# Attention of the first group: scores eight steps ahead of their unit's transposes instead of six

## The chip, the cores and the metric

The kernel runs on one core of a Trainium2 chip. The metric is the device time of one execution in microseconds (us); the median of three runs before the change is 1029.18 us (1029.17 to 1029.4).

## The reference

One layer of a transformer over 1024 tokens of width 1024, all in float32. Two groups of heads share one input projection. Group A is windowed attention with grouped keys and a sink per head, group B is neighbourhood attention on a 16 x 64 grid. After them come an output projection and a gated MLP with a depthwise convolution of width 3.

```python
hn = rmsnorm(h, norm_mix[l])
proj = jnp.einsum('bsd,de->bse', hn, w_in[l])
qa, ka, va, qb, kb, vb = jnp.split(proj, splits, axis=-1)
...
# group A, per block of 128 queries: keys of the blocks before, at and after it
s = jnp.einsum('bqgrd,bkgd->bgrqk', q_i, k_i).astype(jnp.float32) * scale
s = jnp.where(valid[None, None, None], s, -1e30)
m = jnp.maximum(jnp.max(s, axis=-1), sink_gr)
p = jnp.exp(s - m[..., None])
denom = jnp.sum(p, axis=-1) + jnp.exp(sink_gr - m)
o = jnp.einsum('bgrqk,bkgd->bgrqd', p.astype(v_i.dtype), v_i)
...
mix = jnp.concatenate([rmsnorm(o_a, norm_a[l]), rmsnorm(o_b, norm_b[l])], axis=-1)
h = h + jnp.einsum('bse,ed->bsd', mix, w_out[l])
hn = rmsnorm(h, norm_ffn[l])
h = h + conv_gated_mlp(hn, w_gate[l], w_up[l], conv_w[l], conv_b[l], w_down[l])
```

Group A has 8 query heads and 2 heads of keys and values, 64 wide, so four query heads share a key head.

## The kernel before

Activations lie with features on the partitions and tokens along the free axis. Every large product is done as three matmuls on operands split into a high and a low part in a rounded format (`x` is high plus low): high by high, high by low and low by high. These three are one **block** (`block`, L177 to L179, into `pj`); a projection job has 16 blocks, eight for each half of the tokens. TensorE's instructions run in the order in which the program writes them (`manual_schedule`); those of the other engines are put in order by a planner, by priorities and its own model of time, and each engine then runs its queue in that order.

**Filling.** The generator `rest` yields one block at a time of the input projections 3 to 17 and then of the output projection; `fill(n)` writes n blocks. While attention runs, such blocks are written between its steps, so that TensorE has work while VectorE, ScalarE and GpSimd do the softmax. `RATES` says how many blocks go to each stretch of eight units of group A, or of four units of group B.

**Units of group A.** A unit (`unit_window`) is one of two key heads by one of eight blocks of 128 tokens: 16 units. It has four score steps (`q_step`, one for each query head) and two or three transposing steps (`t_step`, one for each block of keys, two for the blocks at the ends). In what follows units are counted from one: the first, the second, and so on.

- A score step writes two matmuls into one of two PSUM banks with tag `s` (L389). VectorE reads the bank, adds the mask and takes the extreme (L412, with `nm` as the result); ScalarE takes the exponential and its sum (L416). Two scores make a pair in one tile `p`. After the second one VectorE takes the reciprocals (L418) and GpSimd scales both halves (L420). GpSimd has before that copied the sinks into two columns of the tile (L411).
- A transposing step takes one block of keys out of all four scores of the unit: four transposes (L452) into a bank with tag `pt`. ScalarE writes its high part `ph` (L426) and VectorE the rest `pl` (L427). The product with the values (L457 with `ph`, L458 with `pl`, into `o`) is written one transposing step later.

Pairs lie in seven tiles in turn: five of tag `p` in the attention pool, and, for the pairs numbered 3 and 6 of each seven (`SPARE`), two of tag `mix` (`pair_tile`).

**The order around the change.** `q_until(u, limit)` hands out the next score steps in order, up to unit u and at most `limit` of them. `FILL0` = 22 blocks are written before any score. Then a first part writes `4 + AHEAD` scores (the first unit's four and `AHEAD` of the second unit's), each followed by one or two blocks in turn, and then a tail of blocks. With six scores this is 9 blocks among them and `FILL1 - 9` = 5 behind them, 14 in all. Then the units take turns. In a unit's turn its transposing steps and products alternate, and four further score steps are put in at the places `EVA` = (1, 3, 5, 8), with blocks after each event. Each such turn of units 1 to 14 takes four scores, so the scores stay the same number ahead of the transposes; from the 15th unit on, all scores up to two units ahead are taken, whatever their number. `run_q` writes blocks beyond the rate if a unit's projections have not been finished when its score is due.

Of the kernel before, what the change touches and what calls it, by code (L numbers as in the profile page):

```python
# [32 lines left out]
FILL0, FILL1 = 22, 14  # L33
RATES = [41, 50, 21, 21, 21, 21, 13, 19, 20, 17]
SPARE = (3, 6)
AHEAD = 2
EVA = (1, 3, 5, 8)
WARM = 8

# [17 lines left out]
def hybrid_layer(tc, xT, w_first, w_in, w_out, w_gate, w_up, w_down, small, sink, rpb, consts, rope, out):  # L57
    nc = tc.nc
    with ExitStack() as ctx:
# [765 lines left out]
        def fill(n):  # L825
            while n > 0 and next(filler, False):
                n -= 1
# [27 lines left out]
        def q_until(u, limit):  # L855
            nonlocal qpos
            res = []
            while qpos < len(queue_q) and queue_q[qpos][0] <= u and len(res) < limit:
                res.append(queue_q[qpos])
                qpos += 1  # L860
            return res

        def run_q(items):
            for u, s in items:
                while any(m not in done for m in flat[u][2]):
                    assert next(filler)
                s()
# [14 lines left out]
        pend = None  # L882
        for i, item in enumerate(q_until(1, 4 + AHEAD)):
            run_q([item])
            fill(i % 2 + 1)
        fill(FILL1 - 9)
        for u in range(len(flat)):
            q, t, need, kind = flat[u]
            if kind == 0 and u < 14:
# [719 lines left out]
```

## Time and profile before

| What | us |
|---|---|
| median of three runs | 1029.18 |
| profiled execution, its own time | 1030.14 |
| its span, from the first to the last instruction | 1028.4 |
| TensorE (PE) busy in the span | 1011.9 |
| VectorE (DVE) busy | 836.6 |
| ScalarE (ACT) busy | 560.6 |
| GpSimd (POOL) busy | 107.7 |

The first scores of group A start at 54 us, its last transposes at 182 us; group B's attention follows up to about 354 us, then the output projection and the MLP. In rows of the profile an instruction is given by its start in us, its length in us, engine, line of the program, operation, output and inputs with their shapes, and `x` with the number of instructions joined in the row. Brackets at the end hold the idle time of the engine before the row, and what released it. A row of a window gives its busy time for PE, PEld (loading of weights), DVE, ACT and POOL, each with a count, then the granted clock of TensorE, the share of DMA and GB/s. SyncE (SP) here only issues DMA. In the table of waits a row says who waited for whom, the total in us, how often, and the longest.

### The profile page before, as it was taken

To read this page: it belongs to the slowest core of one execution; us is meant where nothing else is said; L and a number is where in the kernel's file an instruction comes from. 1 tells how busy PE (TensorE), PEld (TensorE's weight loads), DVE (VectorE), ACT (ScalarE), POOL (GpSimd) and SP (SyncE) were. 2 spreads that over 40 slices of the span, in tenths; PEclk is the share of its full clock that TensorE was granted. 3 is DMA by queue.
4 is the path that set the end of the run, shared out by engine and by line. 5 is a ranking of instruction groups with operands and counts; after the bars stand their busy time and mean duration, and the time that the engine had idled before them with its cause. 6 is when DMAs were issued, how large, how long until landed. Compare 5 with 4: busy or idle time off the path is not lost.

```text
span 1028.4 us, 14846 instructions
## 1 busy us (share of the span) xinstructions
PE 1011.9 (98%) x5094; PEld 889.3 (86%) x5094; DVE 836.6 (81%) x1566; ACT 560.6 (55%) x1077; POOL 107.7 (10%) x188
## 2 busy tenths in 40 slices
PE   9999999999999999999999999999999999999996
PEld 8888888888888888888888888888888888888886
DVE  7889888768888799999987777786787767896765
ACT  8467776657676545565545444443544644554451
POOL 0233332232242100000000000000000000000002
PEclk9999999999999999999999999999999999999998
DMA  7223122333325247313443332233322889866644
GB/s 291 77 77 78 47 72 62 84 81 82 83 61 176 76 164 261 102 50 114 154 185 103 124 121 95 102 113 113 102 111 95 285 281 305 299 237 236 225 149 164
DMA packets 68220, 144.94 MB, mean 141 GB/s; under 512 B 8240, under 2 KB 18736, under 8 KB 68144
## 3 DMA queue, kind: packets, MB, share of 16 engines
q1 hardware_dynamic: 58064, 118.82, 36.0%
q10 hardware_dynamic: 10080, 25.17, 6.3%
q8 instruction: 40, 0.66, 0.3%
q14 instruction: 36, 0.29, 0.1%
HBM read 103.58 MB, written 28.57 MB: 129 GB/s over the span
## 4 chain that ended last, share of the span: by engine, by line
PE 77%; DVE 13%; ACT 4%; DMA 3%; issue 2%; SPq 0%; POOL 0%; DVEq 0%; ACTq 0%; POOLq 0%
PE dn L994 6%; PE dn L992 6%; PE dn L993 6%; PE x L992 6%; PE x L993 6%; PE x L994 6%; PE pj L177 5%; PE pj L178 5%; PE pj L179 5%; PE y L992 3%; PE y L993 3%; PE y L994 3%; PE s L389 3%; PE z L993 2%; PE z L992 2%
## 5 line engine op out<-in xcount | busy, mean ns | idle before, releaser
L992 PE MATMUL x<-hg,whi 128*128 128x512 f32 x352 | 133.7, 380 | 1.2 <-ACT gs L1034 1.2
L993 PE MATMUL x<-hg,whi 128*128 128x512 f32 x352 | 133.4, 379 | 0.0
L994 PE MATMUL x<-hg,wlo 128*128 128x512 f32 x352 | 133.4, 379 | 0.0
L992 PE MATMUL dn<-xd,whi 128*128 128x512 f32 (+1 forms) x330 | 120.8, 366 | 0.0
L993 PE MATMUL dn<-xd,whi 128*128 128x512 f32 (+1 forms) x330 | 120.5, 365 | 0.0
L994 PE MATMUL dn<-xd,wlo 128*128 128x512 f32 (+1 forms) x330 | 120.5, 365 | 0.0
L416 ACT ACTIVATE p<-p,nm 128x385 f32<-128x385 f32 (+3 forms) x128 | 74.9, 586 | 53.8 <-DVE nm L412 50.3
L177 PE MATMUL pj<-xgh,whi 128*128 128x512 f32 x245 | 99.9, 408 | 0.7 <-ACT xgh L637 0.4
L966 ACT ACTIVATE whi<-ws 128x512 fp32r<-128x512 f32 (+1 forms) x100 | 60.7, 621 | 71.9 <-DVE ws L1106 16.5
L420 POOL TENSOR_SCALAR p<-p,sm 128x384 f32<-128x384 f32 (+1 forms) x128 | 78.7, 628 | 198.9 <-DVE sm L418 159.4
L178 PE MATMUL pj<-xgl,whi 128*128 128x512 f32 x245 | 93.0, 379 | 0.3 <-DVE xgl L638 0.3
L179 PE MATMUL pj<-xgh,wlo 128*128 128x512 f32 x245 | 92.9, 379 | 0.0
L966 ACT ACTIVATE whi<-raw 128x512 fp32r<-128x512 f32 (+1 forms) x102 | 60.9, 611 | 44.1 <-PE x L993 20.0
L967 DVE TENSOR_TENSOR wlo<-ws,whi 128x512 fp32r<-128x512 f32 (+1 forms) x100 | 66.6, 679 | 20.1 <-ACT whi L966 19.9
L427 DVE TENSOR_TENSOR pl<-pt,ph 128x384 fp32r<-128x384 f32 (+2 forms) x108 | 63.3, 589 | 20.5 <-ACT ph L426 18.3
L1314 ACT ACTIVATE xd<-xd 128x512 fp32r<-128x512 f32 x77 | 47.5, 626 | 54.5 <-DMA xd<-x 54.0
L992 PEld LDWEIGHTS x<-hg,whi 128*128 128x128 f32 x352 | 66.5, 189 | 11.4 <-ACT gs L1034 2.0
L1315 DVE TENSOR_TENSOR xd<-xd 128x512 fp32r<-128x512 f32 x77 | 52.2, 686 | 29.6 <-ACT xd L1314 29.3
L1429 POOL TENSOR_TENSOR h<-h,wide 128x256 f32<-128x256 f32 (+1 forms) x6 | 5.4, 915 | 672.0 <-ACT wide L1425 672.0
L994 PEld LDWEIGHTS x<-hg,wlo 128*128 128x128 f32 x352 | 66.5, 189 | 9.4
L993 PEld LDWEIGHTS x<-hg,whi 128*128 128x128 f32 x352 | 66.5, 189 | 9.4
L992 PEld LDWEIGHTS dn<-xd,whi 128*128 128x128 f32 x330 | 62.5, 189 | 7.7
(267 smaller groups left out, 2531.7 us busy)
## 6 DMA issues: line engine op xcount, KB each, us to landing
xd<-x SPq DMA_DIRECT2D x77, 256.0 KB, 5.3
raw<-in_w_down_dram SPq DMA_DIRECT2D x72, 256.0 KB, 4.1
raw<-in_w_gate_dram SPq DMA_DIRECT2D x22, 512.0 KB, 3.5
raw<-in_w_up_dram SPq DMA_DIRECT2D x22, 512.0 KB, 3.5
x<-c ACTq DMA_DIRECT2D x22, 512.0 KB, 2.6
raw<-in_w_in_dram SPq DMA_DIRECT2D x30, 256.0 KB, 2.8
raw<-in_w_down_dram SPq DMA_DIRECT2D x36, 192.0 KB, 4.4
x<-t ACTq DMA_DIRECT2D x11, 512.0 KB, 2.6
```

The costliest lines, as they stand in the source:

```text
L177: nc.tensor.matmul(ps, w[0], mv(x[0][:, tsl(h)]), start=first, stop=False)
L178: nc.tensor.matmul(ps, w[0], mv(x[1][:, tsl(h)]), start=False, stop=False)
L179: nc.tensor.matmul(ps, w[1], mv(x[0][:, tsl(h)]), start=False, stop=last)
L416: nc.scalar.activation(p[:, j, 0:e], p[:, j, 0:e], AF.Exp, bias=nm, scale=-1.0, accum_out=sm[:, j:j + 1])
L420: nc.gpsimd.tensor_scalar(p[:, i, 0:m], p[:, i, 0:m], sm[:, i:i + 1], 1.0, op0=ALU.mult, op1=ALU.mult)
L427: mark["rest"] = nc.vector.tensor_tensor(pl[:, 0:n], ps[:, 0:n], f32(ph[:, 0:n]), op=ALU.subtract)
L966: nc.scalar.activation(hi, src, AF.Copy)
L967: nc.vector.tensor_tensor(lo, src, f32(hi[:, :, :]), op=ALU.subtract)
L992: nc.tensor.matmul(ps, w[0], x[0], start=first and i == 0, stop=False, skip_group_check=True)
L993: nc.tensor.matmul(ps, w[0], x[1], start=False, stop=False, skip_group_check=True)
L994: nc.tensor.matmul(ps, w[1], x[0], start=False, stop=last and i == len(ws) - 1, skip_group_check=True)
L1315: nc.vector.tensor_tensor(lo, f32(lo), f32(hi), op=ALU.subtract)
```

## The change

`AHEAD` goes from 2 to 4, so the first part writes eight scores, the first and the second unit's, and each unit's turn writes scores that lie eight steps ahead of its own transposes. The first part then has 12 blocks among its scores, and the tail behind it is cut from five blocks to two, so that 14 blocks are written before the first transposes as before. No instruction is added or taken away.

```diff
-AHEAD = 2
+AHEAD = 4
...
         for i, item in enumerate(q_until(1, 4 + AHEAD)):
             run_q([item])
             fill(i % 2 + 1)
-        fill(FILL1 - 9)
+        fill(FILL1 - 12)
         for u in range(len(flat)):
             q, t, need, kind = flat[u]
             if kind == 0 and u < 14:
```

## The prediction

> **What bounds the kernel now.** I read the page first, then the busy time by stages, the waits of TensorE, and last the engines' instructions in order of time around every stop of TensorE in the first group's attention (54 to 182 us).
>
> ```profile
> span 1028.4 us, 14846 instructions
> PE 1011.9 (98%) x5094; PEld 889.3 (86%) x5094; DVE 836.6 (81%) x1566; ACT 560.6 (55%) x1077; POOL 107.7 (10%) x188
> 60.00:70.00 10.00, 10.00 (x58) 8.97 (x57) 7.59 (x20) 5.91 (x14) 4.21 (x7) 1.00 0.35 98
> 100.00:110.00 10.00, 9.08 (x51) 7.53 (x51) 9.60 (x28) 8.06 (x23) 4.12 (x8) 1.00 0.44 106
> 110.00:120.00 10.00, 10.00 (x62) 9.00 (x61) 7.58 (x26) 6.56 (x20) 3.17 (x9) 1.00 0.08 27
> 54.00:182.00 128.00, 126.62 (x716) 112.73 (x716) 110.06 (x321) 90.83 (x233) 44.78 (x91) 1.00 0.25 67
> PE pt L452 <- POOL p L420: 0.8, 2, 0.6
> PE s L389 <- DVE nm L412: 0.5, 1, 0.5
> ```
>
> Rows by window give window, length, then busy us of PE, PEld, DVE, ACT and POOL, the granted clock, and DMA. TensorE's stream is written out by hand and it is busy 98% of the span at a clock of 1.00, so the time can move only by what TensorE now loses by waiting. The change keeps every matmul, so the whole question is the stops. In the first group's 128 us TensorE is idle for only 128.00 - 126.62 = 1.38 us. The waits of 60 to 110 us name two causes: transposes (L452) that wait for GpSimd's scaling of `p` (L420), and one score that waits for VectorE to read its bank.
>
> Idle time understates a stop here, because a matmul's shown end overlaps the next start. So I take stops from the distance between starts:
>
> ```profile
> 98.85 0.60 PE L452 MATMUL pt<-cst,p 128*128 128x128 f32 x4
> 99.21 0.41 PE L389 MATMUL s<-ka,q 128*128 128x384 f32 x1
> ...
> 100.70 0.38 PE L452 MATMUL pt<-cst,p 128*128 128x128 f32 x2
> 101.68 0.33 PE L452 MATMUL pt<-cst,p 128*128 128x128 f32 x1 [0.60 <-POOL p L420]
> 102.24 0.33 PE L452 MATMUL pt<-cst,p 128*128 128x128 f32 x1 [0.23 <-POOL p L420]
> 102.33 0.46 PE L177 MATMUL pj<-xgh,whi 128*128 128x512 f32 x1
> ...
> 108.92 0.91 PE L452 MATMUL pt<-cst,p 128*128 128x128 f32 x4
> 109.58 0.46 PE L177 MATMUL pj<-xgh,whi 128*128 128x512 f32 x1
> 130.49 0.80 PE L452 MATMUL pt<-cst,p 128*128 128x128 f32 x4
> 131.05 0.41 PE L389 MATMUL s<-ka,q 128*128 128x384 f32 x1
> 154.08 0.79 PE L452 MATMUL pt<-cst,p 128*128 128x128 f32 x4
> 154.63 0.46 PE L177 MATMUL pj<-xgh,whi 128*128 128x512 f32 x1
> ```
>
> Four transposes that find their input ready take 99.21 - 98.85 = 0.36 us. The first four of the sixth unit take 102.33 - 100.70 = 1.63, a loss of 1.27. The same sum at 108.92, 130.49 and 154.08 (first transposes of the seventh, tenth and thirteenth unit) gives 0.66, 0.56 and 0.55, losses of 0.30, 0.20 and 0.19. Together 1.96 us: everything that the wait for scaled `p` costs in this group.
>
> The Trainium skill, "Perfetto Trace Analysis", section Tensor Engine Instruction, says the end of a TensorE instruction is computed by the profiler and not observed. The trace agrees: by the idle column the first stop is 0.60 + 0.23 = 0.83 us, by starts 1.27, and the three others do not appear as idle at all; a sum by idle time alone would stop at 0.83.
>
> Why the sixth unit waits is read backwards from 100.70:
>
> ```profile
> 97.28 0.60 DVE L412 CUSTOM_DVE_ANT_0 p<-s,cst,nsink 128x384 f32<-128x384 f32 x1
> 99.73 0.61 ACT L416 ACTIVATE p<-p,nm 128x385 f32<-128x385 f32 x1
> 100.79 0.16 DVE L418 RECIPROCAL sm<-sm 128x2 f32<-128x2 f32 x1
> 95.59 1.15 POOL L420 TENSOR_SCALAR p<-p,sm 128x384 f32<-128x384 f32 x2 [2.99 <-DVE sm L418]
> 101.04 1.15 POOL L420 TENSOR_SCALAR p<-p,sm 128x384 f32<-128x384 f32 x2 [1.45 <-DVE sm L418]
> ```
>
> The reduce of the unit's fourth score starts at 97.28, its exponential at 99.73 (ScalarE did other work first), the reciprocal at 100.79, and the scaling of the pair ends at 101.04 + 1.15 = 102.19, when the transposes have already stood for over a microsecond. The row at 95.59 scales the pair before it.
>
> **The change, part by part.** *Steady part.* Each unit's turn still issues four scores at the same four places of the stream; two complete a pair each, at the same places as before. So each engine has the same work at the same place; only the pair it belongs to is later by one. The last pair of a unit is therefore scaled where its first pair is scaled now: for the sixth unit by 95.59 + 1.15 = 96.74 and not 102.19, 3.96 us ahead of the transposes at 100.70. All four losses go: -1.96 us.
>
> *What is late next.* VectorE is busy 9.60 of 10 us where the first two stops lie and has no room to follow a faster TensorE there:
>
> ```profile
> 101.92 0.69 DVE L427 TENSOR_TENSOR pl<-pt,ph 128x512 fp32r<-128x512 f32 x1
> 103.60 0.38 PE L458 MATMUL o<-pl,v 128*128 128x512 f32 x1
> 109.31 0.68 DVE L427 TENSOR_TENSOR pl<-pt,ph 128x512 fp32r<-128x512 f32 x1
> 110.75 0.38 PE L458 MATMUL o<-pl,v 128*128 128x512 f32 x1
> ```
>
> The product at 103.60 needs the rest `pl` that ends at 101.92 + 0.69 = 102.61, a margin of 0.99. TensorE would arrive 1.27 earlier and wait 0.28; it carries 0.99 on. The stop at 108.92 adds 0.30, so 1.29. The product at 110.75 needs the `pl` that ends at 109.99: margin 0.76, so 0.53 more goes back and 0.76 is left. From 110 to 120 VectorE is busy only 7.58 of 10 us, so nothing more is taken, and 0.20 + 0.19 at the later stops are kept. Net: -1.96 + 0.28 + 0.53 = -1.15 us. Bounds: nothing given back, -1.96; all of the first two stops given back, -0.39. I take the middle value since both margins are read from rows, though VectorE's order may shift by an instruction.
>
> *Prelude.* Two scores (the second unit's last) move ahead of the first transposes, with the three filling blocks that stood in the tail of five. Before the first transposes there are 14 blocks either way: 9 + 5 before, 12 + 2 after. The two scores bring two reduces, two exponentials, a reciprocal and a scaling ahead of the first `ph` and `pl`:
>
> ```profile
> 62.45 0.17 DVE L418 RECIPROCAL sm<-sm 128x2 f32<-128x2 f32 x1 [0.78 <-ACT p L416]
> 66.09 0.29 DVE L265 TENSOR_TENSOR f<-f,turns 128x128 f32<-128x128 f32 x1 [1.43 <-DMA f<-t]
> 66.16 0.60 ACT L426 ACTIVATE ph<-pt 128x512 fp32r<-128x512 f32 x1 [2.56 <-PE pt L452]
> ```
>
> VectorE stands idle for 0.78 and 1.43 us there and ScalarE for 2.56. Two reduces at 0.60 (the row at 97.28) and a reciprocal at 0.16 make 1.36, inside 2.21; two exponentials at 0.61 make 1.22, inside 2.56. TensorE loses nothing in 60 to 70 us (10.00 of 10). So 0. If that cover were gone, 1.36 us of VectorE work would stand before the first `pl`: between 0 and +1.36. I take 0, since the idle stands just where the scores would land.
>
> *The one wait of a score, in the third unit's turn.* Reduces per unit are unchanged, so I keep it. Bounds: -0.46 (its idle) to 0.
>
> ```profile
> 80.98 0.43 PE L389 MATMUL s<-ka,q 128*128 128x384 f32 x1 [0.46 <-DVE nm L412]
> ```
>
> *Buffers and the end of the group.* Pairs live in seven tiles, five of tag `p` and two spare. At most five were in use at once; now six. A pair takes the tile of the pair seven before it, whose last transposes now lie half a unit nearer, but still in the unit before: 0. In the fifteenth unit two scores are left for four, since the second group's first two are issued earlier; the projections that the ninth unit and the second group need are done by block count well before (by block 52 where 66 have run, and by 84 where 114 have), so no block is pulled forward: 0. No score of this group issues a DMA, and no transfer changes its place on SyncE's queue.
>
> *A port rule, weighed.* GpSimd's scaling meets VectorE:
>
> ```profile
> 107.86 1.58 POOL L420 TENSOR_SCALAR p<-p,sm 128x384 f32<-128x384 f32 x2 [3.33 <-PE pt L452]
> 102.52 0.68 DVE L170 TENSOR_TENSOR wlo<-raw,whi 128x512 fp32r<-128x512 f32 x1
> 108.07 0.91 DVE L170 TENSOR_TENSOR wlo<-raw,whi 128x512 fp32r<-128x512 f32 x1
> ```
>
> The scaling of two at 107.86 took 1.58 and not 1.15, and the weight split that began inside it 0.91 and not 0.68. One such meeting more costs VectorE 0.23, which is within the bounds above. The Trainium skill, "SBUF — State Buffer", section Who interferes with whom, says a VectorE instruction with two SBUF inputs and a GpSimd instruction that reads SBUF block one another. It speaks against moving scalings; by it the sum would be at worst -1.15 + 2 x 0.23 = -0.69 if both pairs moved ahead in the prelude met a split there.
>
> **Sum.** The profiled execution took 1030.14 us (a span of 1028.4 and 1.74 around it), 0.96 above the median of the runs, 1029.18. Against its own time: 1030.14 - 1.15 = 1028.99. For the median: 1029.18 - 1.15 = 1028.03, so 1028.0, with -1.96 to -0.39, 1027.2 to 1028.8, as this case's own range.
>
> **Rivals.** *More than the sum:* nothing is given back and the score's wait goes too, since two reduces are done early: -1.96 - 0.46 = -2.42, 1026.8. For it: VectorE's 2.21 us of idle are used before its busy stretch. Against: its work per unit stays, and both margins above are too short.
>
> *The lead is only on paper:* VectorE's lag simply moves to another wait. All of the first two stops comes back (-0.39), and the prelude's cover fails (+1.36): up to +0.97, 1030.2. For it: 9.60 of 10 us busy. Against: 7.58 just after.
>
> *Slower, by GpSimd's queue.* Its queue runs in order and holds the sink copies (L411), which wait for a tile to be freed by transposes:
>
> ```profile
> 68.42 1.27 POOL L411 COPY p<-nsink 128x2 f32<-128x2 f32 x2 [4.57 <-PE pt L452]
> 69.67 1.15 POOL L420 TENSOR_SCALAR p<-p,sm 128x384 f32<-128x384 f32 x2
> 92.29 0.31 POOL L411 COPY p<-nsink 128x2 f32<-128x2 f32 x2
> ```
>
> At 68.42 a copy stood 4.57 us for transposes with a scaling behind it. With six of seven tiles in use, the copy waits for a unit's last transposes; scalings queued behind it start only then. From the fifth unit's last transposes (98.85) to the sixth's first (100.70) lie 1.85 us: room for 0.36 of transposes, 0.31 of copies and one scaling of a pair, 1.15 (1.82). It decides from the second pair behind a copy: 0.36 + 0.31 + 2.30 - 1.85 = 1.12 lost per unit. In six of the twelve units from the third on that is 6.7 - 2.0 = +4.7, 1033.9; from four units (4.5 - 2.0 = +2.5) it is slower by over 0.2%. Against it: a pair has a unit's time before it is needed, and the planner has so far put copies where nothing urgent stands behind.
>
> **How the numbers follow.** 0.2% of 1029.18 is 2.06 us, about what a measurement of this kernel can tell from no change. Forecast (-0.39 to -1.96) 0.47; more than the sum 0.18, faster; only on paper 0.16; slower by GpSimd's queue 0.19. So faster 0.18, within 0.2% 0.63, slower 0.19. The range goes from 1026.7 to 1030.2 (the three first cases, the low end widened by 0.1, since idle understates the score's wait) and leaves out the last.
>
> **What would show it.** Right: the first transposes of the sixth, seventh, tenth and thirteenth unit follow in 0.36 us and the wait of L452 for L420 is gone; a wait of `o` for `pl` (L458 on L427) appears at the sixth or seventh unit; 60 to 70 us stays at 10.00 busy; the wait of L389 at the third unit stays. Wrong: L452 still waiting for GpSimd, with L411 ahead of L420 in its queue; idle before 70 us; or a difference after 190 us, where I expect the same stream shifted by one constant.

## The result and the profile after

The changed kernel took 1027.84 us (median of 22 runs), the kernel before 1029.36 us (median of 22 runs beside them). The ratio is 0.9985, with a 95% interval of 0.9978 to 0.9991: 1.5 us faster (0.9 to 2.3). On another occasion the same kernel gave 0.9981 (0.9972 to 0.9989). The forecast was 1028.0 in 1026.7 to 1030.2, and within 0.2% of the time before.

The profiled execution of the changed kernel took 1027.14 us, 3.0 less than that of before. This pair of profiles overstates the gain: the two differ at the start and in the MLP, which also differ between repeats of one kernel. From the first matmul of L992, in the MLP, to the end the changed kernel took 611.9 us in one profile and 612.8 in another. The attention does not have this scatter, so the experiments below are read there.

The busy time by stages of the changed kernel, and then the waits of TensorE (50 to 110 us; us in total, times, longest):

```profile
60.00:70.00 10.00, 10.00 (x58) 9.05 (x58) 8.41 (x24) 6.83 (x17) 3.69 (x7) 1.00 0.37 103
100.00:110.00 10.00, 9.90 (x59) 8.66 (x58) 9.11 (x31) 8.09 (x22) 4.88 (x10) 1.00 0.30 77
54.00:182.00 128.00, 127.75 (x725) 114.09 (x724) 110.41 (x327) 92.77 (x238) 44.35 (x91) 1.00 0.25 66
```

```profile
PE s L389 <- DVE nm L412: 0.2, 1, 0.2
```

TensorE's idle time from 54 to 182 us fell from 1.38 to 0.25 us. The wait of L452 for GpSimd's L420 is gone from the table. In 60 to 70 us VectorE is busy 8.41 us where it was 7.59: the two scores that moved ahead. TensorE lost nothing there.

The first transposes of the sixth, seventh, tenth and thirteenth unit, and what follows them, in TensorE's instructions in order of time; and GpSimd's scaling of the sixth unit's last pair:

```profile
101.05 0.60 PE L452 MATMUL pt<-cst,p 128*128 128x128 f32 x4
101.41 0.46 PE L177 MATMUL pj<-xgh,whi 128*128 128x512 f32 x1
...
107.79 0.60 PE L452 MATMUL pt<-cst,p 128*128 128x128 f32 x4
108.15 0.46 PE L177 MATMUL pj<-xgh,whi 128*128 128x512 f32 x1
...
129.63 0.60 PE L452 MATMUL pt<-cst,p 128*128 128x128 f32 x4
129.98 0.41 PE L389 MATMUL s<-ka,q 128*128 128x384 f32 x1
...
153.25 0.60 PE L452 MATMUL pt<-cst,p 128*128 128x128 f32 x4
153.61 0.46 PE L177 MATMUL pj<-xgh,whi 128*128 128x512 f32 x1
95.87 1.16 POOL L420 TENSOR_SCALAR p<-p,sm 128x384 f32<-128x384 f32 x2 [2.85 <-DVE sm L418]
```

All four take 0.35 or 0.36 us, where they took 1.63, 0.66, 0.56 and 0.55. The pair that the sixth unit waited for is scaled by 95.87 + 1.16 = 97.03, 4.0 us ahead of its transposes (3.96 were forecast). The whole 1.96 us of this wait went.

What came in its place, again in TensorE's order, with the VectorE instruction behind each:

```profile
80.67 0.38 PE L458 MATMUL o<-pl,v 128*128 128x512 f32 x1
80.92 0.43 PE L389 MATMUL s<-ka,q 128*128 128x384 f32 x1
...
89.15 0.60 PE L452 MATMUL pt<-cst,p 128*128 128x128 f32 x4
89.90 0.43 PE L389 MATMUL s<-ka,q 128*128 128x384 f32 x1 [0.15 <-DVE nm L412]
89.23 0.61 DVE L412 CUSTOM_DVE_ANT_0 p<-s,cst,nsink 128x384 f32<-128x384 f32 x1
...
109.10 0.38 PE L457 MATMUL o<-ph,v 128*128 128x512 f32 x1
109.58 0.48 PE L458 MATMUL o<-pl,v 128*128 128x512 f32 x1
109.90 0.38 PE L177 MATMUL pj<-xgh,whi 128*128 128x512 f32 x1
108.84 0.68 DVE L427 TENSOR_TENSOR pl<-pt,ph 128x512 fp32r<-128x512 f32 x1
...
148.69 0.60 PE L452 MATMUL pt<-cst,p 128*128 128x128 f32 x4
149.25 0.43 PE L389 MATMUL s<-ka,q 128*128 128x384 f32 x1
...
174.97 0.46 PE L457 MATMUL o<-ph,v 128*128 128x512 f32 x1
175.36 0.48 PE L458 MATMUL o<-pl,v 128*128 128x512 f32 x1
175.68 0.38 PE L177 MATMUL pj<-xgh,whi 128*128 128x512 f32 x1
```

The score's wait of the third unit's turn is nearly gone: 80.92 - 80.67 = 0.25 for a step of 0.22. Four new stops stand against it, all for VectorE by what they follow:

- 89.90 - 89.15 = 0.75 less 0.36, so 0.39: a score whose bank is read by the reduce at 89.23.
- 109.58 - 109.10 = 0.48 less 0.22, so 0.26: the product for the `pl` that ends at 109.52. The step behind it is longer too, 109.90 - 109.58 = 0.32 for 0.22, so 0.36 in all.
- 149.25 - 148.69 = 0.56 less 0.36, so 0.20: a score again.
- 175.68 - 174.97 = 0.71 for the two products behind a group of transposes, where the same place takes 0.51 in the kernel with eight steps and no scaling (below), so 0.20. The `pl` of this product ends at 175.30.

Together 1.15 us.

Beyond the first group there is one more difference, at the second transposes of the next values, with the kernel before first and the changed kernel second:

```profile
186.36 0.60 PE L334 MATMUL vt<-cst,t 128*128 128x128 f32 x4
187.30 0.45 PE L177 MATMUL pj<-xgh,whi 128*128 128x512 f32 x1 [0.34 <-DVE v L339]
```

```profile
184.88 0.60 PE L334 MATMUL vt<-cst,t 128*128 128x128 f32 x4
185.32 0.45 PE L177 MATMUL pj<-xgh,whi 128*128 128x512 f32 x1
```

The distance fell from 187.30 - 186.36 = 0.94 to 0.44 us, another 0.50; undisturbed it would be 0.36. After it the two streams run at a constant distance through the rest of attention.

### The profile page after: what moved, and what is told of

It reads as the page before. It is cut to its first block, busy times and chain, and to the rows that moved or that the text cites. A ratio compares the mean times of both kernels' runs of the same rounds, so it can differ in the third digit from the quotient of the medians.

```text
span 1025.3 us, 14859 instructions
## 1 busy us (share of the span) xinstructions
PE 1011.5 (99%) x5094; PEld 890.5 (87%) x5094; DVE 836.6 (82%) x1566; ACT 562.0 (55%) x1077; POOL 108.6 (11%) x188
## 4 chain that ended last, share of the span: by engine, by line
PE 84%; DVE 10%; ACT 4%; issue 2%; DMA 1%; DVEq 0%; POOL 0%; ACTq 0%; POOLq 0%
PE dn L994 7%; PE dn L992 7%; PE dn L993 6%; PE pj L177 6%; PE pj L178 6%; PE pj L179 6%; PE x L992 6%; PE x L993 6%; PE x L994 6%; PE y L994 3%; PE y L993 3%; PE y L992 3%; PE s L389 3%; PE z L994 2%; PE z L992 2%
## 5 line engine op out<-in xcount | busy, mean ns | idle before, releaser
L992 PE MATMUL x<-hg,whi 128*128 128x512 f32 x352 | 133.6, 380 | 0.9 <-ACT gs L1034 0.9
L992 PE MATMUL dn<-xd,whi 128*128 128x512 f32 (+1 forms) x330 | 120.8, 366 | 0.0
L420 POOL TENSOR_SCALAR p<-p,sm 128x384 f32<-128x384 f32 (+1 forms) x128 | 79.7, 635 | 204.6 <-DVE sm L418 177.8
L992 PEld LDWEIGHTS x<-hg,whi 128*128 128x128 f32 x352 | 66.5, 189 | 10.9 <-ACT gs L1034 1.5
L992 PEld LDWEIGHTS dn<-xd,whi 128*128 128x128 f32 x330 | 62.5, 189 | 7.7
```

The costliest lines, as they stand in the source:

```text
L420: nc.gpsimd.tensor_scalar(p[:, i, 0:m], p[:, i, 0:m], sm[:, i:i + 1], 1.0, op0=ALU.mult, op1=ALU.mult)
L992: nc.tensor.matmul(ps, w[0], x[0], start=first and i == 0, stop=False, skip_group_check=True)
```

## The experiments

For a comparison free of the scatter at the start I take the distance between two marks that every kernel has: the first value transposes of all, near 60 us, and those near 222 us. Here they are for the kernel before, then for the changed one:

```profile
60.76 1.04 PE L334 MATMUL vt<-cst,t 128*128 128x128 f32 x8
223.85 0.60 PE L334 MATMUL vt<-cst,t 128*128 128x128 f32 x4
```

```profile
60.63 1.04 PE L334 MATMUL vt<-cst,t 128*128 128x128 f32 x8
221.88 0.60 PE L334 MATMUL vt<-cst,t 128*128 128x128 f32 x4
```

That is 163.09 and 161.25 us. The same difference for each kernel, beside the ratio of its times to the kernel before run beside it:

| kernel | between the marks | against 163.09 | time ratio (95%) |
|---|---|---|---|
| before, again | 163.14 | +0.05 | 1.0000 (0.9991 to 1.0009) |
| changed | 161.25 | -1.84 | 0.9985 (0.9978 to 0.9991) |
| changed, again | 161.17 | -1.92 | 0.9981 (0.9972 to 0.9989) |
| first part only | 162.72 | -0.37 | 0.9987 (0.9978 to 0.9996) |
| first part only, again | 162.66 | -0.43 | 0.9989 (0.9980 to 0.9998) |
| turns only | 161.36 | -1.73 | 0.9977 (0.9968 to 0.9986) |
| six ahead, no scaling | 161.18 | -1.91 | 0.9977 (0.9968 to 0.9985) |
| six ahead, double scaling | 168.69 | +5.60 | 1.0049 (1.0035 to 1.0062) |
| eight ahead, double scaling | 162.89 | -0.20 | 0.9996 (0.9987 to 1.0005) |
| eight ahead, no scaling | 160.64 | -2.45 | 0.9978 (0.9969 to 0.9987) |
| seven ahead | 162.72 | -0.37 | 0.9993 (0.9984 to 1.0002) |
| ten ahead | 161.95 | -1.14 | 0.9988 (0.9979 to 0.9996) |
| eight ahead, old end | 160.94 | -2.15 | 0.9974 (0.9963 to 0.9985) |

Where a kernel was profiled twice, the two distances agree within 0.08 us, while its times have intervals of 0.6 us and more to either side. The distances carry the verdicts on the attention. Of the time outside the marks they say nothing.

Two theories stood against each other. By the **lead** theory the gain is that a unit's last pair is scaled half a unit earlier. By the **early-work** theory it is that VectorE does two reduces in idle time, ahead of its busy stretch.

**The first part alone.** The changed kernel, but scores run eight ahead only until the first unit's turn.

```diff
-                mine = q_until(u + 2, 4)
+                mine = q_until(u + 2, 2 if u == 0 else 4)
```

> The first part writes eight scores with 12 blocks among them and 2 behind, as in the change, but the first unit's turn takes two scores instead of four, so from the second turn on scores are six steps ahead as before. Lead theory (the gain is that a unit's last pair is scaled half a unit earlier, so its transposes no longer wait): no gain, time of before within 0.5 us, the first transposes of the sixth, seventh, tenth and thirteenth unit wait for L420 again. Early-work theory (the gain is that VectorE does two reduces in its idle before 66 us, ahead of its busy stretch): the gain of the change, -1.5 us, or most of it.

The stretch shortened by 0.37 us, the time by 1.35 us (0.4 to 2.3). The stretch fits the lead theory and the time the early-work theory, so the kernel was run again, with the kernel before and the changed one as controls.

> The first part alone once more. Its first profile shows 0.4 us gained between 58 and 200 us, its times 1.35 us. Lead theory: the profile is right, and the rest is scatter at the start and in the MLP; time between 0 and -0.8 us. Early-work theory: -1.0 to -1.5 us again, and over 1 us gained between 58 and 200 us in the profile.

> The kernel before once more, as a control: time within 0.4 us of before by either theory, and a second profile that shows which stops repeat. Lead theory: the stops of L452 on L420 at the sixth, seventh, tenth and thirteenth unit repeat within 0.3 us each. Rival (the first profile's stops were that run's chance): they lie elsewhere.

> The changed kernel once more: -1.0 to -2.0 us against before. In its attention (58 to 200 us) both theories expect the gain of the first profile, 1.85 us, within 0.4.

Both readings repeated. The distances were -0.43 for the first part alone, +0.05 for the kernel before and -1.92 for the changed one; the time of the first part alone was 1.4 us shorter again (0.2 to 2.1), beyond the 0 to 0.8 of the lead theory, though the interval reaches into it. All four stops of L452 returned at the same places in both kernels without the lead. TensorE's waits for GpSimd in the first part alone (second profile, 50 to 200 us), and its fourth and sixth unit:

```profile
PE pt L452 <- POOL p L420: 0.6, 3, 0.2
```

```profile
85.67 0.67 PE L452 MATMUL pt<-cst,p 128*128 128x128 f32 x3
86.58 0.33 PE L452 MATMUL pt<-cst,p 128*128 128x128 f32 x1 [0.23 <-POOL p L420]
86.66 0.41 PE L389 MATMUL s<-ka,q 128*128 128x384 f32 x1
...
100.61 0.38 PE L452 MATMUL pt<-cst,p 128*128 128x128 f32 x2
101.15 0.33 PE L452 MATMUL pt<-cst,p 128*128 128x128 f32 x1 [0.16 <-POOL p L420]
101.72 0.33 PE L452 MATMUL pt<-cst,p 128*128 128x128 f32 x1 [0.23 <-POOL p L420]
101.80 0.46 PE L177 MATMUL pj<-xgh,whi 128*128 128x512 f32 x1
```

The sixth unit's stop is smaller, 101.80 - 100.61 - 0.36 = 0.83 where it was 1.27, and the score's wait in the third unit's turn (0.61) is gone. Against these stands a fifth stop of L452, at the fourth unit, which the kernel before does not have: 86.66 - 85.67 - 0.36 = 0.63. Net, early work is worth about 0.4 us of 1.9 between the marks. The times of this kernel, 0.9987 and 0.9989, lie nearer to the changed kernel's than its stretch does, yet both intervals reach down to 0.4 us or less. The rest lies in the MLP: from the first matmul of L992 to the end its two profiles took 611.7 and 611.5 us, those of the kernel before 612.9 and 612.7. Whether this is scatter, as between the two profiles of the changed kernel, or comes of the edit is open.

**The turns alone.** The first part stays at six scores, and the first unit's turn takes six.

```diff
-EVA = (1, 3, 5, 8)
+EVA = (1, 3, 5, 8, 9, 10)
...
-                mine = q_until(u + 2, 4)
+                mine = q_until(u + 2, 6 if u == 0 else 4)
```

> The first part writes six scores as before (9 blocks and 5), and the first unit's turn takes six scores instead of four (the two more at its end), so that scores run eight steps ahead from the second turn on. Lead theory: the change's gain, -1.0 to -1.9 us, no wait of L452 for L420 from the sixth unit on. Early-work theory: no gain or slower (0 to +1 us), since VectorE gets the two reduces in its busy stretch and not in its idle.

The stretch shortened by 1.73 us. The table of waits (50 to 200 us) has one row left:

```profile
PE o L458 <- DVE pl L427: 0.2, 1, 0.2
```

The lead alone, without the longer first part, gives nearly all of the gain between the marks, and the score's wait in the third unit's turn is gone here too. The first part of the change is only one way to get there.

**The scaling taken away.** Kernel before; GpSimd's scaling is left out in group A.

```diff
                     for i, m in enumerate(st["n"]):
-                        nc.gpsimd.tensor_scalar(p[:, i, 0:m], ...)
+                        if nsink is None:
+                            nc.gpsimd.tensor_scalar(p[:, i, 0:m], ...)
```

> The kernel before with GpSimd's scaling (L420) left out for the first group, so its probabilities are not divided by their sum; reciprocals stay. Lead theory: the four waits of L452 for L420 cannot occur, a pair is ready when its exponential is; -1.2 to -1.9 us against before, about the change's own gain. Early-work theory: the waits only move to ScalarE's exponential and VectorE's rest; within 0.5 us of before.

-1.91 us with six steps of lead, about the gain of the lead. The two are not quite the same thing: without scaling VectorE is faster as well (the weight splits, L170, take 685 ns on average where they took 759), and other stops are left. So this run fits the lead theory, but the size alone does not prove it.

**The scaling doubled**, six and eight ahead.

```diff
                         nc.gpsimd.tensor_scalar(p[:, i, 0:m], p[:, i, 0:m], sm[:, i:i + 1], 1.0, ...)
+                        if nsink is not None:
+                            nc.gpsimd.tensor_scalar(p[:, i, 0:m], p[:, i, 0:m], 1.0, 1.0, ...)
```

> The kernel before with the scaling of the first group followed by a second pass over the same pair (times 1.0) on GpSimd, so a pair is ready about 1.15 us later. Lead theory: most units' first transposes stand with less than 1.15 us of margin, so about 6 us slower (4 to 10), with a wait of L452 for L420 at most units. Early-work theory: the wait for a pair is not what decides; under 2 us slower.

> The changed kernel with the same second pass on GpSimd. Lead theory: the margin of about 4 us covers 1.15; within 0.7 us of the changed kernel (1027.1 to 1028.8), no wait of L452 for L420. Early-work theory: as much slower against the changed kernel as the same edit makes the kernel before.

Six ahead: +5.60 us, as forecast by the lead theory, though by starts eight of the sixteen units wait and not most of them. (The edit moves the transposes to L454 and the scaling to L422; six ahead first, then eight ahead, from the tables of waits for 50 to 200 us.)

```profile
PE pt L454 <- POOL p L422: 5.5, 11, 1.4
```

```profile
PE s L389 <- DVE nm L412: 1.0, 3, 0.4
PE o L460 <- DVE pl L429: 0.2, 1, 0.2
```

Eight ahead, no transposes wait for GpSimd: the lead covers a second scaling. But the stretch is 1.64 us longer than the changed kernel's, where the lead theory allowed 0.7 and the early-work theory asked for 5.6: both missed. The waits are for VectorE. Its groups by line (54 to 182 us), the changed kernel first, then the one with the double scaling; the number behind the busy time is the mean ns of one:

```profile
L427 DVE TENSOR_TENSOR pl<-pt,ph 128x512 fp32r<-128x512 f32 x43 | 29.6, 689 | 5.6 <-ACT ph L426 4.4
L170 DVE TENSOR_TENSOR wlo<-raw,whi 128x512 fp32r<-128x512 f32 x14 | 10.0, 716 | 0.4 <-ACT whi L169 0.3
L307 DVE SCALAR_TENSOR_TENSOR kb<-t,cst,ka 128x512 fp32r<-128x512 f32 x4 | 3.0, 747 | 0.0
L278 DVE SCALAR_TENSOR_TENSOR t<-t,q 128x512 fp32r<-128x512 f32 x4 | 2.6, 684 | 0.0
```

```profile
L429 DVE TENSOR_TENSOR pl<-pt,ph 128x512 fp32r<-128x512 f32 x43 | 29.6, 688 | 5.4 <-ACT ph L428 4.4
L170 DVE TENSOR_TENSOR wlo<-raw,whi 128x512 fp32r<-128x512 f32 x13 | 9.6, 738 | 0.3 <-ACT whi L169 0.3
L307 DVE SCALAR_TENSOR_TENSOR kb<-t,cst,ka 128x512 fp32r<-128x512 f32 x4 | 3.2, 809 | 0.0
L278 DVE SCALAR_TENSOR_TENSOR t<-t,q 128x512 fp32r<-128x512 f32 x4 | 3.2, 828 | 0.0
```

Three groups of VectorE whose two input tensors both lie in SBUF became slower: 684 to 828 ns, 747 to 809, 716 to 738, in all 4 x 0.144 + 4 x 0.062 + 13 x 0.022 = 1.1 us. The one that reads a PSUM bank and one tile (`pl`) stayed at 689 and 688. The Trainium skill, "SBUF — State Buffer", section Who interferes with whom, says that a VectorE instruction with two SBUF inputs contends with a GpSimd instruction that reads SBUF, and these rows agree. Whether the 1.1 us make up the 1.64 us was not tested by itself.

**Eight ahead without scaling** (the edit of the scaling taken away, on the changed kernel).

> The changed kernel with GpSimd's scaling left out for the first group (its probabilities are not divided by their sum). Lead theory: the lead already covers the scaling, so within 0.4 us of the changed kernel in attention (1.5 to 2.3 us gained against before). If GpSimd's scaling costs the changed kernel time in another way (by slowing VectorE's instructions that it meets): over 0.4 us better than the changed kernel.

-2.45 us, 0.6 us better than the changed kernel by the distance; the times do not tell the two apart. No wait of TensorE is left in the table of waits. By starts the stop at 109.58 fell from 0.36 to 0.18 and that at 149.25 from 0.20 to 0.02, the one at 175.36 is gone, and the one at 89.90 is left. The weight splits of VectorE, 716 ns in the changed kernel, take 683:

```profile
L170 DVE TENSOR_TENSOR wlo<-raw,whi 128x512 fp32r<-128x512 f32 x14 | 9.6, 683 | 0.5 <-ACT whi L169 0.4
```

So GpSimd's scaling costs the changed kernel something beside the pair's readiness, and the weight splits are slower with it. That this alone makes the 0.6 us was not tested.

**Seven ahead.**

```diff
-AHEAD = 2
+AHEAD = 3
...
-        fill(FILL1 - 9)
+        fill(FILL1 - 10)
```

> Seven scores in the first part (10 blocks among them, 4 behind), so seven steps ahead. A unit's last score moves from the second to the first of the four places in the turn before it, about 1.4 us earlier; worked out from the profile of before, its pair is then scaled by about 99.4, 106.7, 127 and 152 us, ahead of the transposes at 100.70, 108.92, 130.49 and 154.08. Lead theory: the four waits are gone already, 1.0 to 1.9 us gained in attention. Early-work theory (one reduce earlier instead of two): half the change's gain or less, under 1.0 us.

```profile
PE s L389 <- DVE nm L412: 0.7, 2, 0.4
PE o L458 <- DVE pl L427: 0.5, 2, 0.2
```

This is the lead theory's miss; the early-work theory's forecast fits the size. The waits of L452 for L420 are all gone, as worked out, but the stretch is only 0.37 us shorter, for VectorE is waited for at six places by starts (the four in this table of 50 to 200 us and two of about 0.2 us, at 97.91 and 150.21, too small for it). With the steps behind late products they cost 2.6 us, where the changed kernel's four cost 1.15. With an odd number of steps the pairs are completed at the first and third place of a turn and no longer at the second and fourth, so VectorE's and GpSimd's order is another one in every unit. That this order causes the new waits is argued from the program and was not tested by itself. The lead removes one wait; VectorE decides how much of the time is kept.

**Ten ahead.** All seven tiles of pairs are in use.

```diff
-AHEAD = 2
+AHEAD = 6
...
-        for i, item in enumerate(q_until(1, 4 + AHEAD)):
+        for i, item in enumerate(q_until(2, 4 + AHEAD)):
             run_q([item])
-            fill(i % 2 + 1)
-        fill(FILL1 - 9)
+            fill(1 if i == 9 else i % 2 + 1)
+        fill(FILL1 - 14)
...
-                mine = q_until(u + 2, 4)
+                mine = q_until(u + 3, 4)
```

> Ten scores in the first part (14 blocks among them, none behind), and each turn takes scores up to three units ahead; all seven tiles of pairs are then in use. Lead theory: nothing is left to gain by lead, so within 0.5 us of the change in attention (1.4 to 2.4 us gained). Rival of the prediction (GpSimd's queue stands at sink copies for a free tile): now that no tile is spare, L411 waits for transposes and L452 for L420; slower than the change by 1 us or more.

```profile
PE s L389 <- DVE nm L412: 0.2, 1, 0.2
PE o L458 <- DVE pl L427: 0.2, 1, 0.2
```

-1.14 us: 0.7 us behind the changed kernel, and short of the lead theory's 1.4 to 2.4, but by waits for VectorE, not for GpSimd (50 to 200 us). L452 does not wait for L420, so sink copies that stand for a free tile cost TensorE nothing even with none to spare. Ten steps brought less than eight; nine were not tried.

**Eight ahead with the old end** (an edit of the changed kernel).

```diff
-                mine = q_until(u + 2, 4)
+                mine = q_until(u + 2, 2 if u == 13 else 4)
```

> The changed kernel, but the fourteenth turn takes two scores instead of four, so that the fifteenth turn has four scores again, as before the change, and only the turns before it run eight ahead. Theory A (the half microsecond that the changed kernel gains at the value transposes near 185 us comes from the lighter fifteenth turn): that stop is back at 0.7 us, and the gain in attention (58 to 200 us) falls from 1.9 to 1.4 us. Theory B (it comes from the time gained before): the stop stays at 0.2 us and the gain at 1.9 us.

The distance at the value transposes near 185 us stayed at 0.44 us (less a step of 0.22, the 0.2 of the theories) though the fifteenth turn had four scores again, so the lighter turn is not its cause (theory A falls). The stretch is the shortest of the kernels that compute everything, 0.3 us shorter than the changed kernel's; the stop at 175.36 (0.20 us) is not there. Its time ratio, 0.9974 (0.9963 to 0.9985), beats the kernel before; against the changed kernel the intervals overlap, so only one profile says that it is better.

## Why the prediction was right, point by point

- *Four waits for scaled pairs, -1.96.* Right in place and size: each of the four fell to 0.36 us. The doubled scaling shows that the pair's readiness was the cause: six steps ahead it brings such waits at eight units and +5.60 us, eight steps ahead it brings none.
- *What is late next, +0.28 and +0.53 at the products with `pl`.* The kind was right, since VectorE took part of the gain back, but neither the places nor the size: 1.15 us and not 0.81. The product of the sixth unit did not wait. That of the seventh waited 0.26, half of what was forecast, and cost 0.36. The rest came at 89.90, ahead of the stops that were removed, and at 149.25 and 175.36, where the forecast had nothing more taken.
- *The prelude, 0.* Right: no idle, 10.00 of 10 us. Early work even brought a net 0.4 us, which the first part alone shows. The forecast had it only in the rival "more than the sum".
- *The wait of a score in the third unit's turn, kept at 0.* Wrong: the 0.61 us by starts fell to 0.03, so 0.58 was gained. The rival "more than the sum" had this wait going, because of early reduces; but it goes in the kernel with turns only too, which moves no reduce ahead of the first transposes. The new stop at 89.90 is of the same kind and is counted above.
- *After 190 us the same stream, shifted.* Right after 186 us, as far as the MLP, but the step itself missed 0.50 us: the distance at the value transposes got shorter. It is 0.44 or 0.45 us in all kernels with seven or more steps of lead, in the one with turns only and in the one with six ahead and double scaling, 0.73 with six ahead and no scaling, and 0.97 with the first part only. It goes with how late VectorE is: its first subtraction of the values (L339) starts 1.05 us after the first value transposes in all kernels with 0.44, 1.35 us in the one with 0.73, and 1.56 to 1.60 us in the kernel before and with the first part only. What makes VectorE late there is not settled.
- *Buffers and GpSimd's queue.* Right: with seven of seven tiles in use no transposes waited for GpSimd. The sink copies (L411) stood for transposes less, not more: 13.2 us in all from 50 to 200 us before, 6.4 in the changed kernel, 2.9 with ten steps. The rival "slower, by GpSimd's queue" is refuted there.
- *The port rule, weighed.* Two scores make one pair, so one pair moved ahead in the prelude and not two. The weight splits took 759 ns on average from 54 to 182 us before and 716 after, so they lost less time to GpSimd and not more.
- *Only on paper.* This rival did not happen at eight steps, but it is much of what seven steps did: the waits go and VectorE's take their place.

By their own terms the stops between 60 and 184 us sum to -1.96 - 0.58 + 1.15 = -1.39 us. The two value transposes at 184.30 and 182.82 give 123.54 and 122.19 us after the first mark, so -1.35. With the 0.50 behind them the sum is -1.89, for the -1.84 and -1.92 of the profiles. So the main term and the direction of the forecast were earned, but that its -1.15 lies near the 1.5 us of the times is partly luck: it left out gains of 0.58 and 0.50, and counted 0.34 too little given back.

## What to carry to other kernels

When the busiest engine waits for the end of a chain over several engines, look how far ahead of its use the chain is started; moving its start costs no work, and the margin can be read from the rows before. Then look at which engine is nearly as busy, since it decides how much is kept: the same wait was removed by seven, eight and ten steps, and the gain was 0.4, 1.9 and 1.1 us. Measure such small effects between two marks inside the profile as well as by times, and repeat the kernel before as a control.

## What the runs showed of the hardware

Between the two marks repeated profiles of one kernel agreed within 0.08 us in 163 (163.09 and 163.14; 161.25 and 161.17; 162.72 and 162.66), while the median times of the kernel before ranged from 1029.04 to 1029.80 us over the occasions, three of which used three different chips. The scatter lies outside the attention: from the second mark to the first matmul of L992 all fourteen profiles took 191.5 or 191.6 us, but the first mark came at 60.03 to 60.78 us, and from L992 to the end it took 611.4 to 613.7 us.

With GpSimd's scalings doubled, three groups of VectorE's instructions with two SBUF inputs were 3 to 21% slower on average (716 to 738, 747 to 809, 684 to 828 ns), and the one with a PSUM input stayed as it was (689 and 688). With the scalings left out, the weight splits went from 716 to 683 ns.
